# Differences of weights, convolution and recurrence in the first mixer on VectorE, the recurrence's constants on GpSimd

## The chip, the cores and the metric

The kernel runs on one core of a Trainium2 chip. The metric is device time in microseconds (us), taken as the median of three runs of the whole program. Beside it stands one profiled execution, whose trace gives the time of single instructions. The engines are named as the profile names them: PE is TensorE, DVE is VectorE, ACT is ScalarE, POOL is GpSimd, SP is SyncE (which here only issues transfers), PEld is TensorE's load of weights.

## What is computed

Two layers, each a token mixer and a squared-ReLU feed-forward block, on one sequence of 1024 tokens with 1024 features. Before every block the activations are normalised and then scaled and shifted by vectors that come from a conditioning vector `c` (adaLN). The first layer's mixer is the one that matters here, a Griffin recurrent block:

```python
u = h @ w_in
xb, gb = jnp.split(u, 2, axis=-1)
gate = jax.nn.gelu(gb)
xc = conv(xb, conv_w) + conv_b                      # 4 taps along the sequence, per feature
r = sigmoid(blockwise(xc, wr) + br)
i = sigmoid(blockwise(xc, wi) + bi)
log_a = -8 * r * softplus(-lam)
a = exp(log_a)
b = sqrt(-expm1(2 * log_a)) * (i * xc)
hs = scan(hs * a + b)                               # along the sequence
return (hs * gate) @ w_out
```

Everything is float32. D_RNN is 1280, in five blocks of 256 features.

## The kernel before

Activations lie transposed, 128 features on the partitions and 512 tokens (one half of the sequence) along a tile. A float32 product is made of three products of a shorter type, fp32r: a value v is split into vh, its rounding, and vl = v - vh, the **difference**, and `mm3` (lines 351 to 353) adds wh·xh, wh·xl and wl·xh. So each weight tile and each activation that goes into a product costs a rounding, always on ACT, and a difference on some other engine. Which engine makes the difference is the subject of this case:

- `weights` (line 334) loads a raw tile of 128x1024 by SP (line 325; three buffers), rounds it on ACT (line 328), and makes the difference on POOL or DVE, by a rotating list `self.lo`: `[1]`, which holds during the first layer, is POOL every time. Differences that are needed a second time are written to memory (line 346) and loaded again for the second half (line 330).
- `startup` computes the scale A0 and shift S0 of the first norm by eight steps kt. In each, `mac` (lines 551, 553) is a chain of eight DVE operations on 128x128 tiles, which PE transposes (line 566) to give the shift (line 569); `cols` (lines 560, 563) gives the scale. Then `apply1` with `first=True` makes the normalised input: a product on POOL (line 97), two scalings on ACT (98, 99), a difference on DVE (100). The differences of these first weights are POOL's too (line 581).
- `mixer0` runs by a list of steps, `plan`: "c" is a convolution (`conv`), "g" a gate, "l" the recurrence (`lru`), "o" the output projection (`oproj`), with the block and the half. Between steps, one or two DVE operations of a later conditioning vector are put in (line 458). `conv` drains a product out of PSUM by three DVE operations (642), rounds it on ACT (647) and makes the difference on POOL (648). `lru` ends with a chain on DVE: 696, 697, a square root on ACT (699), 703, the scan (705), the gate (708), then the rounding on ACT (710) and the difference on POOL (711). `oproj` multiplies that and adds into the activations on DVE (729), which frees the PSUM buffer.
- `lru_params` makes the constants of the recurrence, some 30 tiny operations on tiles of 128x10 and 128x20, nearly all on DVE (lines 390 to 416).

The order on each engine is not the order of the code: a scheduler sorts the instructions of all steps and engines when the program is built, and each engine then works through its own list strictly in order. An instruction that waits holds up all that stand behind it on its engine.

Of the kernel before, what the change touches and what calls it, by code (L numbers as in the profile page):

```python
# [9 lines left out]
FT = mybir.dt.float32  # L10
# [37 lines left out]
class Norm:  # L48
# [39 lines left out]
        else:  # L88
            self.rstd = ps

    def apply1(self, kt, A, sh, first=False):
        T, nc = self.T, self.T.nc
        t = T.nshort()
        hh, hl = T.tileR(), T.tileR()
        a, b = A[:, kt:kt + 1], sh[:, kt:kt + 1]
        if first:
            nc.gpsimd.tensor_tensor(t, T.x[self.h, kt], self.rstd, op=OP.mult)
            nc.scalar.activation(hh, t, AF.Identity, bias=b, scale=a)
            nc.scalar.activation(t, t, AF.Identity, bias=b, scale=a)
            nc.vector.tensor_tensor(hl, t, hh.bitcast(FT), op=OP.subtract)  # L100
        else:
            nc.vector.scalar_tensor_tensor(t, T.x[self.h, kt], a, self.rstd, op0=OP.mult, op1=OP.mult)  # L102
            nc.scalar.activation(hh, t, AF.Identity, bias=b)  # L103
            nc.vector.scalar_tensor_tensor(hl, t, b, hh.bitcast(FT), op0=OP.add, op1=OP.subtract)  # L104
        return hh, hl

    def apply(self, A, sh):
# [95 lines left out]
class Trunk:  # L203
# [182 lines left out]
    def lru_params(self):  # L386
        nc, col = self.nc, self.col

        hb = self.const.tile([P, 20], FT, name="hb")
        nc.vector.tensor_scalar(hb, col[:, 186:206], 0.5, None, op0=OP.mult)  # L390
        self.hbr = lambda k: hb[:, k:k + 1]
        self.hbi = lambda k: hb[:, 10 + k:11 + k]

        lam = col[:, 206:216]
        v = nc.vector
        w = [self.small([P, 10], f"sp{k}", 1) for k in range(6)]
        ab, u, z, z2, acc, mx = w
        v.tensor_scalar(ab, lam, -1.0, None, op0=OP.mult)
        v.tensor_tensor(ab, ab, lam, op=OP.max)
        nc.scalar.activation(u, ab, AF.Exp, scale=-1.0)  # L400
        v.tensor_scalar(z, u, 2.0, None, op0=OP.add)
        v.reciprocal(z, z)
        v.tensor_tensor(z, z, u, op=OP.mult)
        v.tensor_tensor(z2, z, z, op=OP.mult)
        v.memset(acc, 1.0 / 17)
        for k in (15, 13, 11, 9, 7, 5, 3, 1):
            v.tensor_tensor(acc, acc, z2, op=OP.mult)
            v.tensor_scalar(acc, acc, 1.0 / k, None, op0=OP.add)
        v.tensor_tensor(acc, acc, z, op=OP.mult)
        v.tensor_scalar(mx, lam, -1.0, 0.0, op0=OP.mult, op1=OP.max)  # L410

        sp = self.const.tile([P, 20], FT, name="sp")
        v.tensor_scalar(acc, acc, 2.0, None, op0=OP.mult)
        v.tensor_tensor(acc, acc, mx, op=OP.add)
        v.tensor_scalar(sp[:, 0:10], acc, 4.0, None, op0=OP.mult)
        v.tensor_scalar(sp[:, 10:20], acc, -4.0, None, op0=OP.mult)
        self.sp = lambda k: sp[:, k:k + 1]
        self.nsp = lambda k: sp[:, 10 + k:11 + k]
# [77 lines left out]
    def startup(self, pool, norm, normb):  # L496
# [77 lines left out]
        mac(0)  # L574
        cols(0)
        for kt in range(KT):
            h.append(norm.apply1(kt, A0, S0, first=True))
            wh = self.wp.tile([P, 768], FR, name=self.nm("wh"), tag="wh")
            wl = self.wp.tile([P, 768], FR, name=self.nm("wl"), tag="wl")
            A.copy(wh, wt[kt][:, 0:768])  # L580
            nc.gpsimd.tensor_tensor(wl, wt[kt][:, 0:768], wh.bitcast(FT), op=OP.subtract)
            if kt + 1 < KT:
                mac(kt + 1)
            for f in range(6):
                if f == 3 and kt + 1 < KT:
                    cols(kt + 1)
                s = slice(f * P, (f + 1) * P)
                self.mm3(acc[f], (wh[:, s], wl[:, s]), h[kt], kt == 0, kt == KT - 1)
# [21 lines left out]
    def mixer0(self, hx, g1, tail, first, plan):  # L610
# [21 lines left out]
        def conv(u, h, pss=None):  # L632
            pss = pss or proj(wcols(u * 256), h)
            for j in range(2):
# [10 lines left out]
                    V.tensor_tensor(y[:, 0:3], y[:, 0:3], edge[:, f], op=OP.add)  # L645
                yh, yl = self.tileR(), self.tileR()
                A.copy(yh, y)
                G.tensor_tensor(yl, y, yh.bitcast(FT), op=OP.subtract)
                xc[u, j], xcs[u, j] = y, (yh, yl)

        def edges():
# [21 lines left out]
        def lru(u, h):  # L673
# [26 lines left out]
            for m in range(2):  # L700
                f = 2 * u + m
                a, b = ab[m]
                V.tensor_tensor(b, b, v[m], op=OP.mult)
                hs = self.tmp("hs")
                V.tensor_tensor_scan(hs, a, b, 0.0 if h == 0 else last[:, f:f + 1], op0=OP.mult, op1=OP.add)
                if h == 0:
                    V.tensor_copy(last[:, f:f + 1], hs[:, HT - 1:HT])
                V.scalar_tensor_tensor(hs, hs, 0.5, gt[u, m], op0=OP.mult, op1=OP.mult)
                yh, yl = self.tileR(), self.tileR()
                A.copy(yh, hs)  # L710
                G.tensor_tensor(yl, hs, yh.bitcast(FT), op=OP.subtract)  # L711
                Y[u, h, m] = (yh, yl)

        def oproj(us, h):
# [543 lines left out]
    def run(self):  # L1258
# [48 lines left out]


        self.layer = 0
        N["m0", 0], N["m0", 1] = Norm(self, 0), Norm(self, 1)  # L1310
        with ExitStack() as st:
            hm[0], first = self.startup(pool(st, "start", 9), N["m0", 0], N["m0", 1])
        F = FFN(self, 0, None, hf)
        with ExitStack() as st:
# [33 lines left out]
                    "g21", "c31", "o011", "l21", "g31", "c41", "l31", "g41", bA, "o21", nA, "l41", f1a, "o341", f1b]  # L1348
            self.mixer0(hm, lambda: mod[0, 2], sqs("f0"), first, plan)
            self.drain()  # L1350


            F.g2, F.tail = mod[0, 5], tail
# [200 lines left out]
```

## Time and profile before

| | |
|---|---|
| median of three runs | 2579.44 us (2574.14 to 2582.48) |
| the profiled execution's own time | 2578.01 us |
| its span, first to last instruction | 2576.2 us |
| PE busy | 2437.7 us, 95% |
| DVE, ACT, POOL busy | 1513.0, 1233.1, 969.9 us |
| mean granted clock of TensorE | 0.978 |

A busy time counts what the engine shows as running, with time in which an instruction has begun and cannot go on. Idle time is put down to what came last of the things waited for. Because PE is busy for nearly the whole span, only the places where it is not matter for the end: the stretch from 0 to 360 us, with the startup, the first half of the mixer and part of the second, is where most of them lie.

### The profile page before, as it was taken

The numbers are of one execution on the slowest core, as the hardware profiler recorded it, in microseconds if no ns is written. First come the engines' busy times: TensorE is split into PE (matmuls) and PEld (weight loads), VectorE is DVE, ScalarE is ACT, GpSimd is POOL, SyncE is SP. The second block draws the span as 40 slices with busy tenths as digits, with TensorE's granted clock in tenths as the row PEclk, the third lists the DMA queues.
The fourth block names the chain that finished last, engine by engine and source line by source line (L and its number), as shares of the span: only waits on it lengthen the run. The fifth ranks groups of instructions, "written<-read, shape, count | busy, mean of one in ns | idle before, by whom it ended". The sixth has DMA issues, their size and how long they took to land. (4 is left out here: it accounts for less than half of the span.)

```text
span 2576.2 us, 30961 instructions
## 1 busy us (share of the span) xinstructions
PE 2437.7 (95%) x10954; PEld 1966.9 (76%) x10954; DVE 1513.0 (59%) x2837; ACT 1233.1 (48%) x2188; POOL 969.9 (38%) x575
## 2 busy tenths in 40 slices
PE   7888999998999999999997999999998999999999
PEld 6666778776788888888776777888886877788887
DVE  6688855788844411376687876555558876321112
ACT  3545565631121133235546767768743974433322
POOL 3455411222122234230137932322325994344442
PEclk8889999999999999999998999999999999999999
DMA  7466566336511378654431431222240104322231
GB/s 238 164 222 202 171 216 227 106 131 222 178 49 47 115 263 298 243 176 164 147 107 30 172 98 64 96 87 90 97 133 9 34 27 146 115 90 97 84 104 60
DMA packets 212285, 342.53 MB, mean 133 GB/s; under 512 B 19658, under 2 KB 123298, under 8 KB 212130
## 3 DMA queue, kind: packets, MB, share of 16 engines
q1 hardware_dynamic: 183184, 295.29, 33.8%
q10 hardware_dynamic: 28946, 45.27, 5.3%
q8 instruction: 86, 1.41, 0.2%
q14 instruction: 69, 0.57, 0.1%
HBM read 274.97 MB, written 65.54 MB: 132 GB/s over the span
## 5 line engine op out<-in xcount | busy, mean ns | idle before, releaser
L334 POOL TENSOR_TENSOR wl<-raw,wh 128x1024 fp32r<-128x1024 f32 (+2 forms) x233 | 572.2, 2463 | 1108.2 <-ACT wh L328 1063.6
L328 ACT CAST wh<-raw 128x1024 fp32r<-128x1024 f32 (+2 forms) x296 | 304.8, 1032 | 584.8 <-PE ps L352 226.5
L351 PE MATMUL ps<-a,wh 128*128 128x512 f32 x1152 | 464.0, 405 | 30.2 <-DVE a L729 12.4
L352 PE MATMUL ps<-a,wh 128*128 128x512 f32 x1152 | 461.1, 400 | 2.9 <-POOL a L711 1.5
L353 PE MATMUL ps<-a,wl 128*128 128x512 f32 x1152 | 459.9, 400 | 0.7 <-DMA wl<-part 0.7
L351 PE MATMUL pd<-a,wh 128*128 128x512 f32 x1072 | 430.1, 402 | 10.5 <-ACT g L667 4.3
L352 PE MATMUL pd<-a,wh 128*128 128x512 f32 x1072 | 430.2, 401 | 7.2 <-DVE a L104 3.7
L353 PE MATMUL pd<-a,wl 128*128 128x512 f32 x1072 | 429.3, 400 | 0.0
L174 DVE SCALAR_TENSOR_TENSOR a<-ps,mod,a 128x512 f32<-128x512 f32 x352 | 259.9, 746 | 262.2 <-PE ps L353 261.5
L351 PEld LDWEIGHTS ps<-a,wh 128*128 128x128 f32 x1152 | 219.5, 191 | 86.1 <-DVE a L729 13.3
L352 PEld LDWEIGHTS ps<-a,wh 128*128 128x128 f32 x1152 | 220.0, 191 | 56.0 <-POOL a L711 2.8
L353 PEld LDWEIGHTS ps<-a,wl 128*128 128x128 f32 x1152 | 219.5, 191 | 54.5 <-DMA wl<-part 1.6
L351 PEld LDWEIGHTS pd<-a,wh 128*128 128x128 f32 x1072 | 203.7, 190 | 62.3 <-issue 5.1
L352 PEld LDWEIGHTS pd<-a,wh 128*128 128x128 f32 x1072 | 204.8, 191 | 58.6 <-DVE a L104 5.0
L353 PEld LDWEIGHTS pd<-a,wl 128*128 128x128 f32 x1072 | 204.5, 191 | 49.2
L1147 POOL TENSOR_SCALAR s<-s,rr 128x128 f32<-128x128 f32 (+7 forms) x128 | 225.8, 1779 | 34.6 <-DVE rr L1145 27.3
L351 PE MATMUL ps<-hid,wh 128*128 128x512 f32 x512 | 204.4, 399 | 11.2 <-DVE a L174 8.0
L352 PE MATMUL ps<-hid,wh 128*128 128x512 f32 x512 | 203.1, 397 | 0.0
L353 PE MATMUL ps<-hid,wl 128*128 128x512 f32 x512 | 203.1, 397 | 0.0
L1025 ACT ACTIVATE signs<-sc,tc 128x384 int8<-128x384 f32 (+5 forms) x186 | 164.0, 882 | 77.6 <-DVE tc L1040 66.4
L458 DVE SCALAR_TENSOR_TENSOR a<-a,cond,a 128x512 f32<-128x512 f32 x140 | 133.0, 983 | 36.7 <-DMA a<-in_ada_w_dram 36.2
L152 DVE TENSOR_TENSOR a<-r,a 128x512 fp32r<-128x512 f32 x64 | 46.9, 754 | 141.6 <-ACT a L151 140.4
(274 smaller groups left out, 3748.9 us busy)
## 6 DMA issues: line engine op xcount, KB each, us to landing
raw<-in_ffn_w_dram SPq DMA_DIRECT2D x192, 512.0 KB, 3.7
a<-in_ada_w_dram ACTq DMA_DIRECT2D x160, 256.0 KB, 3.4
part<-wl SPq DMA_DIRECT2D x69, 512.0 KB, 3.4
wl<-part SPq DMA_DIRECT2D x69, 512.0 KB, 4.1
part<-wh SPq DMA_DIRECT2D x40, 512.0 KB, 2.7
wh<-part SPq DMA_DIRECT2D x40, 512.0 KB, 3.5
raw<-in_a_w_in_dram SPq DMA_DIRECT2D x34, 512.0 KB, 4.3
raw<-in_a_w_out_dram SPq DMA_DIRECT2D x20, 512.0 KB, 4.2
```

Source lines behind the costliest of these rows:

```text
L152: nc.any.tensor_tensor(ql, r, qh.bitcast(FT), op=OP.subtract)
L174: nc.vector.scalar_tensor_tensor(xt, ps, self.g2[:, m:m + 1], xt, op0=OP.mult, op1=OP.add)
L328: nc.scalar.copy(wh, raw)
L334: eng.tensor_tensor(wl, raw, wh.bitcast(FT), op=OP.subtract)
L351: pe.matmul(out, wh, xh, start=start, stop=False)
L352: pe.matmul(out, wh, xl, start=False, stop=False)
L353: pe.matmul(out, wl, xh, start=False, stop=stop)
L458: nc.vector.scalar_tensor_tensor(a, r, s, a, op0=OP.mult, op1=OP.add)
L1025: A.activation(self.signs[:, 0:L], sc, AF.Sign, bias=0.0 if neg is None else neg.bitcast(FT), accum_out=n)
L1147: G.tensor_scalar(sl[e][:, 0:L], sl[e][:, 0:L], r[:, e:e + 1], None, op0=OP.mult)
```

## The change

All of the differences in the first layer up to the end of the mixer are made by DVE: those of the startup's weights (581), of the weights in `weights` (`self.lo` is `[0]` from the start until the mixer is drained, and `[1]` again after), of the convolution (648) and of the recurrence's output (711). `apply1` loses its special form for the first half: it takes the form that all other norms have, two DVE operations and one ACT operation. The tiny operations of `lru_params` go to POOL, 27 of them; three stay on DVE.

```diff
-    def apply1(self, kt, A, sh, first=False):
+    def apply1(self, kt, A, sh):
...
-        if first:
-            nc.gpsimd.tensor_tensor(t, T.x[self.h, kt], self.rstd, op=OP.mult)
-            nc.scalar.activation(hh, t, AF.Identity, bias=b, scale=a)
-            nc.scalar.activation(t, t, AF.Identity, bias=b, scale=a)
-            nc.vector.tensor_tensor(hl, t, hh.bitcast(FT), op=OP.subtract)
-        else:
-            nc.vector.scalar_tensor_tensor(t, T.x[self.h, kt], a, self.rstd, op0=OP.mult, op1=OP.mult)
-            nc.scalar.activation(hh, t, AF.Identity, bias=b)
-            nc.vector.scalar_tensor_tensor(hl, t, b, hh.bitcast(FT), op0=OP.add, op1=OP.subtract)
+        nc.vector.scalar_tensor_tensor(t, T.x[self.h, kt], a, self.rstd, op0=OP.mult, op1=OP.mult)
+        nc.scalar.activation(hh, t, AF.Identity, bias=b)
+        nc.vector.scalar_tensor_tensor(hl, t, b, hh.bitcast(FT), op0=OP.add, op1=OP.subtract)
...
-        nc.vector.tensor_scalar(hb, col[:, 186:206], 0.5, None, op0=OP.mult)
+        nc.gpsimd.tensor_scalar(hb, col[:, 186:206], 0.5, None, op0=OP.mult)
...
-        v = nc.vector
+        v = nc.gpsimd
...
-        v.tensor_tensor(ab, ab, lam, op=OP.max)
+        nc.vector.tensor_tensor(ab, ab, lam, op=OP.max)
...
-        v.reciprocal(z, z)
+        nc.vector.reciprocal(z, z)
...
-        v.tensor_scalar(mx, lam, -1.0, 0.0, op0=OP.mult, op1=OP.max)
+        nc.vector.tensor_scalar(mx, lam, -1.0, 0.0, op0=OP.mult, op1=OP.max)
...
-            nc.gpsimd.tensor_tensor(wl, wt[kt][:, 0:768], wh.bitcast(FT), op=OP.subtract)
+            V.tensor_tensor(wl, wt[kt][:, 0:768], wh.bitcast(FT), op=OP.subtract)
...
-                G.tensor_tensor(yl, y, yh.bitcast(FT), op=OP.subtract)
+                V.tensor_tensor(yl, y, yh.bitcast(FT), op=OP.subtract)
...
-                G.tensor_tensor(yl, hs, yh.bitcast(FT), op=OP.subtract)
+                V.tensor_tensor(yl, hs, yh.bitcast(FT), op=OP.subtract)
...
         self.layer = 0
+        self.lo = [0]
...
             self.drain()
+            self.lo = [1]
```

The scheduler sorts anew. In the changed kernel a line's number is lower by 6 (the scan of line 705 is line 699 there). Two places show what moves.

VectorE, the second recurrence (block 1, first half), before: from the sum for the root (696) to the gated output (708). Names are those of the program, with the buffer's number.

```order
L696 SCALAR_TENSOR_TENSOR v_1191<-v_1191,tg_1223 128x512
L703 TENSOR_TENSOR tg_1208<-tg_1208,v_1191 128x512
L703 TENSOR_TENSOR tg_1232<-tg_1232,v_1191 128x512
L705 SCALAR_TENSOR_TENSOR hs_1242<-la_1210,tg_1208 128x512
L705 SCALAR_TENSOR_TENSOR hs_1251<-la_1234,tg_1232 128x512
L707 COPY hlast<-hs_1242 128x1
L668 SCALAR_TENSOR_TENSOR g_1330<-g_1330,pd_1281 128x512
L708 SCALAR_TENSOR_TENSOR hs_1242<-hs_1242,g_975 128x512
```

VectorE, the same place in the changed kernel.

```order
L328 TENSOR_TENSOR wl_1527<-raw_1523,wh_1526 128x1024
L690 SCALAR_TENSOR_TENSOR v_1183<-v_1183,tg_1215 128x512
L328 TENSOR_TENSOR wl_1563<-raw_1559,wh_1562 128x1024
L697 TENSOR_TENSOR tg_1200<-tg_1200,v_1183 128x512
L697 TENSOR_TENSOR tg_1224<-tg_1224,v_1183 128x512
L699 SCALAR_TENSOR_TENSOR hs_1234<-la_1202,tg_1200 128x512
L699 SCALAR_TENSOR_TENSOR hs_1243<-la_1226,tg_1224 128x512
L701 COPY hlast<-hs_1234 128x1
L460 TENSOR_REDUCE adat_1431<-ps_1432 128x4
L702 SCALAR_TENSOR_TENSOR hs_1234<-hs_1234,g_967 128x512
```

Two differences of weights (L328) now stand ahead of the recurrence's end, one of them where DVE waits for the root on ACT; between the products by the root and the gated output no difference stands.

VectorE, the fourth recurrence (block 3, first half), before: around its scans. L729 frees a PSUM buffer of an output projection, L102 belongs to the second half's norm.

```order
L102 SCALAR_TENSOR_TENSOR ns_2136<-a_851,mod_89,ps_2036 128x512
L703 TENSOR_TENSOR tg_1896<-tg_1896,v_1879 128x512
L703 TENSOR_TENSOR tg_1920<-tg_1920,v_1879 128x512
L705 SCALAR_TENSOR_TENSOR hs_1930<-la_1898,tg_1896 128x512
L705 SCALAR_TENSOR_TENSOR hs_1939<-la_1922,tg_1920 128x512
L707 COPY hlast<-hs_1930 128x1
L668 SCALAR_TENSOR_TENSOR g_2018<-g_2018,pd_1969 128x512
L708 SCALAR_TENSOR_TENSOR hs_1930<-hs_1930,g_1757 128x512
L707 COPY hlast<-hs_1939 128x1
L729 SCALAR_TENSOR_TENSOR a_134<-ps_2052,mod_759,a_134 128x512
```

VectorE, the same place in the changed kernel.

```order
L96 SCALAR_TENSOR_TENSOR ns_2128<-a_843,mod_89,ps_2028 128x512
L723 SCALAR_TENSOR_TENSOR a_134<-ps_2044,mod_751,a_134 128x512
L96 SCALAR_TENSOR_TENSOR ns_2134<-a_850,mod_89,ps_2028 128x512
L697 TENSOR_TENSOR tg_1888<-tg_1888,v_1871 128x512
L697 TENSOR_TENSOR tg_1912<-tg_1912,v_1871 128x512
L699 SCALAR_TENSOR_TENSOR hs_1922<-la_1890,tg_1888 128x512
L699 SCALAR_TENSOR_TENSOR hs_1931<-la_1914,tg_1912 128x512
L701 COPY hlast<-hs_1922 128x1
L662 SCALAR_TENSOR_TENSOR g_2010<-g_2010,pd_1961 128x512
L702 SCALAR_TENSOR_TENSOR hs_1922<-hs_1922,g_1749 128x512
```

The first addition into the activations (L723, before L729), which stood behind both scans, stands ahead of them now.

## Rows read from the trace of the kernel before

**Rows 1.** Page, part 2: busy tenths in 40 slices of 64.4 us, PE and DVE

```profile
PE   7888999998999999999997999999998999999999
DVE  6688855788844411376687876555558876321112
```

**Rows 2.** Table by stretch: stretch, its length, then busy us and instructions by engine, clock

```profile
core 0: us, PE busy (x) PEld busy (x) DVE busy (x) ACT busy (x) POOL busy (x), PEclk, DMA share, GB/s
...
150.00:180.00 30.00, 21.30 (x79) 16.61 (x80) 22.94 (x21) 15.44 (x20) 18.63 (x8) 0.77 0.71 241
...
240.00:270.00 30.00, 20.20 (x76) 14.95 (x74) 27.73 (x32) 14.55 (x20) 15.70 (x7) 0.83 0.48 158
270.00:300.00 30.00, 28.48 (x122) 22.95 (x123) 29.38 (x38) 18.23 (x27) 11.66 (x6) 1.00 0.41 140
...
sum 360.00, PE 305.67 PEld 244.00 DVE 270.59 ACT 183.19 POOL 155.58; mean PE 25.47 PEld 20.33 DVE 22.55 ACT 15.27 POOL 12.96
```

**Rows 3.** Groups on DVE, 0 to 360 us: count, busy us, mean ns, idle before

```profile
L458 DVE SCALAR_TENSOR_TENSOR a<-a,cond,a 128x512 f32<-128x512 f32 x42 | 51.0, 1243 | 14.9 <-DMA a<-in_ada_w_dram 14.8
...
L705 DVE TENSOR_TENSOR_SCAN hs<-la,tg 128x512 f32<-128x512 f32 x10 | 24.7, 2510 | 0.0
...
L697 DVE SCALAR_TENSOR_TENSOR tg<-tg,xc 128x512 f32<-128x512 f32 x12 | 13.2, 1104 | 0.9 <-ACT tg L688 0.9
```

**Rows 4.** Single lines on DVE, whole span: least, median, greatest ns

```profile
L458 DVE SCALAR_TENSOR_TENSOR a<-a,cond,a x140: 734/747/2900, 116.4 to 691.6; 128x512 f32<-128x512 f32 x140
...
L697 DVE SCALAR_TENSOR_TENSOR tg<-tg,xc x20: 679/684/2901, 123.3 to 495.1; 128x512 f32<-128x512 f32 x20
...
L705 DVE TENSOR_TENSOR_SCAN hs<-la,tg x10: 1193/3322/3429, 134.8 to 294.0; 128x512 f32<-128x512 f32 x10
...
L334 DVE TENSOR_TENSOR wl<-raw,wh x34: 834/1226/3122, 1316.7 to 1941.6; 128x1024 fp32r<-128x1024 f32 x31, 128x768 fp32r<-128x768 f32 x2, 128x656 fp32r<-128x656 f32 x1
```

**Rows 5.** Groups on POOL, 0 to 360 us

```profile
L334 POOL TENSOR_TENSOR wl<-raw,wh 128x1024 fp32r<-128x1024 f32 x35 | 92.7, 2663 | 82.5 <-ACT wh L328 62.8 <-DMA a<-in_ada_w_dram 14.3 <-DMA raw<-in_a_gate_i_w_dram 3.5
L648 POOL TENSOR_TENSOR a<-xc,a 128x512 fp32r<-128x512 f32 x14 | 18.5, 1325 | 29.7 <-ACT a L647 24.5 <-ACT halo L639 5.2
L711 POOL TENSOR_TENSOR a<-hs,a 128x512 fp32r<-128x512 f32 x12 | 16.2, 1362 | 42.1 <-ACT a L710 42.1
```

**Rows 6.** Instructions in order of time: start us, duration us; startup, DVE and PE

```profile
17.54 1.85 DVE L551 TENSOR_SCALAR ma<-st,cond 128x128 f32<-128x128 f32 x1
...
23.31 1.96 DVE L553 SCALAR_TENSOR_TENSOR ma<-st,cond,ma 128x128 f32<-128x128 f32 x1
...
26.15 0.34 DVE L553 SCALAR_TENSOR_TENSOR ma<-st,cond,ma 128x128 f32<-128x128 f32 x1
...
28.57 0.48 PE L566 MATMUL ps<-ident,ma 128*128 128x128 f32 x1 [5.71 <-DVE ma L553]
...
31.13 1.22 PE L351 MATMUL pd<-a,wh 128*128 128x512 f32 x2 [0.58 <-ACT a L98]
```

**Rows 7.** In order of time, around PE's longest wait in the mixer, 154 to 175 us

```profile
154.80 2.90 DVE L697 SCALAR_TENSOR_TENSOR tg<-tg,xc 128x512 f32<-128x512 f32 x1
157.62 3.55 DVE L458 SCALAR_TENSOR_TENSOR a<-a,cond,a 128x512 f32<-128x512 f32 x2
...
163.89 8.98 POOL L334 TENSOR_TENSOR wl<-raw,wh 128x1024 fp32r<-128x1024 f32 x3 [3.92 <-ACT wh L328]
...
164.11 6.62 DVE L705 TENSOR_TENSOR_SCAN hs<-la,tg 128x512 f32<-128x512 f32 x2
...
174.12 0.80 PE L351 MATMUL ps<-a,wh 128*128 128x512 f32 x1 [8.70 <-ACT a L710]
```

**Rows 8.** In order of time, around the next long wait, 243 to 256 us

```profile
243.52 2.88 DVE L696 SCALAR_TENSOR_TENSOR v<-v,tg 128x512 f32<-128x512 f32 x1
...
248.84 4.47 DVE L705 TENSOR_TENSOR_SCAN hs<-la,tg 128x512 f32<-128x512 f32 x2
...
255.33 0.79 PE L351 MATMUL ps<-a,wh 128*128 128x512 f32 x1 [7.97 <-DVE a L729]
```

**Rows 9.** Groups on DVE, whole span: differences of weights

```profile
L334 DVE TENSOR_TENSOR wl<-raw,wh 128x1024 fp32r<-128x1024 f32 x31 | 44.0, 1420 | 25.2 <-ACT wh L328 25.0
```

More of the change, by code (lines that the diff above doesn't have):

```diff
@@ L576, in startup @@
         for kt in range(KT):
-            h.append(norm.apply1(kt, A0, S0, first=True))
+            h.append(norm.apply1(kt, A0, S0))
             wh = self.wp.tile([P, 768], FR, name=self.nm("wh"), tag="wh")
```

## The prediction, made before the changed kernel ran

> **What bounds the kernel now.** I read the slices first [rows 1]. PE is at 9 tenths or more nearly everywhere; its weakest run of slices is the first four, which end at 258 us, and in these DVE is at 6 to 8 tenths. The second view is the table by stretch [rows 2]: over the first 360 us PE is busy 305.67 us, so it stands idle for 54.3, and DVE is busy 270.59, so it has 89.4 us free. The holes are not spread evenly. From 150 to 180 us PE is busy 21.30 of 30, from 240 to 270 it is 20.20, and in just these two the granted clock is low, 0.77 and 0.83, where the stretch from 270 to 300 has 1.00. So a hole costs more than its length: when PE comes back after it, its products run at the lower of its two levels (1.2 GHz instead of 2.4) for some microseconds.
>
> Third, what the holes wait for, in order of time. The longest ends at 174.12: PE waited 8.70 us for ACT's rounding of the second recurrence's output [rows 7]. The next ends at 255.33: 7.97 us for an addition on DVE (L729) that frees a PSUM buffer and stood behind two scans [rows 8]. Both end in a chain on DVE, and the last view says why that chain is slow. One scan takes 1.19 us at the least, but 3.32 in the median, and the mean over the first 360 us is 2.51 [rows 3, 4]. The operation of L458 is the same every time and takes 0.747 in the median, 2.900 at most; over the first 360 us the mean is 1.243. What happens in the long ones is seen at one place: from 163.89 POOL works 8.98 us at three differences of weights, and two scans that begin at 164.11 take 6.62 [rows 7]. DVE's operations with two inputs from SBUF begin, and then stand until a POOL instruction is through. So in this stretch much of DVE's busy time is standing, and it is POOL's differences that it stands for.
>
> **The change, part by part.** *VectorE's load.* Added over the first 360 us [rows 5]: 35 differences of 128x1024, 14 of L648, 12 of L711, and in the startup 8 of 128x768 and 8 operations more in `apply1`. On DVE a difference of 128x1024 takes 1.226 us (L334, median), an operation of 128x512 0.684 (L697, median) [rows 4]; for 128x768 I take the middle, 0.95. That is 35 x 1.226 + 34 x 0.684 + 8 x 0.95 = 73.8 us. Given back is the standing: L458 42 x (1.243 - 0.747) = 20.8, the scans 10 x (2.51 - 1.193) = 13.2, L697 12 x (1.104 - 0.684) = 5.0 [rows 3, 4], so 39 us from three groups alone. L553, L696, L703 and others show the same long cases among their short ones (1.96 beside 0.34 for L553 [rows 6], 2.88 for L696 [rows 8]); I estimate 30 for them. And some 27 tiny operations leave. So DVE's load stays about the same, within 10 us either way, and that by itself brings nothing. What changes is where it lies: DVE's chains become as short as their own operations, and the differences stand elsewhere in the order.
>
> *Startup.* The first product in full begins at 31.13 us. It needs the first shift, hence the chain of eight (L551, L553), which began at 17.54 and was through at 28.57, though one link costs 0.34 [rows 6]: 3 us of work in 11. Two links took 1.85 and 1.96 beside POOL's operations, and the tiny operations stood in between. Now POOL has only tiny ones then. The gain is at most 11 - 3 = 8, less what stands in the chain's way now (one operation of `apply1`, 0.68, and one difference of 0.95); and POOL's 27 tiny operations can still hold DVE, each briefly. ACT's chain is one operation shorter in each of the eight steps. I take 5 (bounds: -2, if the tiny ones hold each link, and 8).
>
> *The hole to 174.12.* In the chain before it, L697 took 2.90, two of L458 3.55, two scans 6.62 [rows 7]; at the medians and the least scan of rows 4 they are 0.68, 1.49 and 2.39, so 8.5 us go. In the same piece of the order there stand now two differences of weights and one of a convolution, 2 x 1.226 + 0.684 = 3.1, one of them while DVE waits for the root. The output comes 5.4 to 6.6 us sooner, and PE's 8.70 fall to about 3; of the time at the low clock about 2 us go with it (the first product after the hole takes 0.80, and the stretch's clock is 0.77 [rows 2]). Gain 8 (bounds 0 and 11).
>
> *The hole to 255.33.* L696 took 2.88, the two scans 4.47 [rows 8], so 2.2 and 2.1 us of standing, with an L458 of the same kind ahead of them. More important is the order: the addition that PE waits for stands ahead of the scans now. PE gets on with the next piece, of six products, and then waits for the second addition, behind the scans. Of 7.97 I take 5, and 2 for the clock (0.83): 7 (bounds 0 and 10).
>
> *The rest to 360 us.* What remains of the 54.3 is the first 30 us, which wait for data, and some ten waits of 1 to 4 us. From 270 to 300 DVE is busy 29.38 of 30 [rows 2], so it is the bound there, and there the standing is the largest part of L458. I take 4 (bounds 0 and 12).
>
> *The price.* A difference waits for ACT's rounding. On POOL that held up only POOL, which had time: 82.5 us idle ahead of the weights' differences alone [rows 5]. On DVE it holds up everything behind. Where DVE makes such differences already, later in the program, it stood idle 25.2 us for 31 of them [rows 9], 0.8 each. 77 are moved within the first 360 us: 62 us, which the 89.4 of idle time can hold, but not at every place. I take 3 (bounds 0 and the rival's 42).
>
> *Behind 360 us.* The order of PE is the same from the end of the mixer on, apart from names, and PE is at 9 tenths; what is gained stays gained. What the 18 differences that follow cost or give I put at nothing: DVE is at 5 tenths in the two slices up to 451 us, which hold most of them [rows 1].
>
> Sum: 5 + 8 + 7 + 4 - 3 = 21. The profiled execution took 2578.01, of which 1.8 lie outside its span; it is 1.4 below the median of the runs, 2579.44. So 2578 - 21 = **2557**. A measurement of this kernel tells 0.3%, 7.7 us, from no change.
>
> **The rivals.** *1. VectorE's order stalls (slower).* The place is the list of DVE between 90 and 360 us: each difference stands at the head and waits for a rounding, which waits for a raw tile, and the additions and drains that free PE's buffers stand behind. It decides from where the waits take all of the idle time and the gain: (89.4 + 24) / 77 = 1.5 us each. At 1.7 each, 131 - 89 - 24 = 18 us are lost: **2596**. For it: 29.38 of 30 busy at 270 to 300 [rows 2], and L648 and L711 follow a rounding that ACT makes just before. Against: 0.8 each where it can be seen [rows 9], and the scheduler puts other work between. In the same direction goes a rule of the Trainium skill (Perfetto Trace Analysis, section "Optimizing Scalar/DVE Operations"): a saturated DVE is a reason to take work off it, even to GpSimd. By that rule alone, with no relief, DVE would have 73.8 us more to do than before and nearly fill the stretch. The section adds that the two share a read port of SBUF, so that moving work between them may not help; the row that decides is the scan of 2.51 against 1.19 [rows 3, 4], which shows the sharing, and so I don't give this more weight than 0.1.
>
> *2. The holes form again elsewhere.* DVE's load is the same, so PE may wait for it just as long at other places; only the startup's 5 stays: **2573**. For it: DVE's sum, above. Against: the two long holes hang on chains of a few operations, not on a sum, and one of them is undone by the order itself.
>
> *3. The holes close.* The holes to 174 and 255 go entirely with their clock (11 + 10), the startup gives 8, the rest 10: 39 us, **2539**. For it: POOL's differences were slow too (2.66 us for 1.23), and what waits for them comes sooner, the loads of the raw tiles among them. Against: DVE is nearly full at 270 to 300.
>
> **How the numbers follow.** The forecast has 0.53, by its own bounds 2546 to 2568; rival 1 0.10, rival 2 0.17, rival 3 0.20. Faster by over 0.3%, that is under 2571.7: nearly all of the forecast (0.51), rival 3, and a third of rival 2 (0.06): 0.77. Slower: rival 1, 0.10. The rest, 0.13, is no difference. The range for 8 in 10 reaches from rival 3's better half to beyond rival 2: 2537 to 2577.
>
> **What would show it.** Right: over the first 360 us the mean of a scan falls to about 1.2 and of L458's operation to about 0.75, DVE's busy time stays within 10 us of 270, POOL's falls under 20; the wait for the second recurrence's output is under 4 us, and the clock of that stretch is over 0.9; the first full product begins before 29 us. Wrong: the means fall and PE's idle time to the end of the mixer does not (rival 2), or DVE's idle time ahead of L334, L648 and L711 is over 1.5 us each (rival 1); or the scans stay long, and then it was not POOL that they stood for.

## The result and the profile after

The changed kernel took 2551.82 us (median of four runs, 2549.04 to 2558.93), the kernel before beside it 2580.96 (four runs, 2574.14 to 2584.48). The ratio is 0.9895 with a 95% interval of 0.9877 to 0.9913: 29 us faster, with an interval of 22 to 32. The forecast was 2557, in a range from 2537 to 2577.

The profiled execution of the changed kernel is the slowest of its four, 2558.93 (span 2557.0); the profiled one of before took 2578.01. So the two traces show 19 of the 29 us, and of the rest they can say nothing.

The slices of the changed kernel, PE and DVE, against [rows 1]:

```profile
PE   7998999999999999999987999999998999999999
DVE  5888775788643412566677876555558875321212
```

In the first four slices PE has 7 9 9 8 where it had 7 8 8 8, and DVE 5 8 8 8 where it had 6 6 8 8. The stretches that answer to [rows 2]:

```profile
core 0: us, PE busy (x) PEld busy (x) DVE busy (x) ACT busy (x) POOL busy (x), PEclk, DMA share, GB/s
150.00:180.00 30.00, 30.00 (x133) 24.05 (x132) 28.48 (x44) 14.05 (x21) 0.00 (x0) 1.00 0.49 159
240.00:270.00 30.00, 19.77 (x70) 15.47 (x70) 28.25 (x42) 16.79 (x23) 0.00 (x0) 0.77 0.26 83
270.00:300.00 30.00, 28.80 (x123) 22.90 (x122) 18.29 (x28) 11.31 (x16) 0.00 (x0) 1.00 0.66 226
0.00:360.00 360.00, 319.00 (x1392) 257.08 (x1393) 273.26 (x481) 191.24 (x283) 12.57 (x36) 0.94 0.65 214
```

Over 360 us PE is busy 13.3 us more, DVE 2.7 us more, and POOL has 12.57 us left of 155.58. DVE got through 481 instructions in that time (405 before, by the same view). The stretch from 150 to 180 has no hole and a clock of 1.00; the stretch from 240 to 270 has a hole as long as before (PE busy 19.77 us where it was 20.20).

DVE's groups over the first 360 us, the first three against [rows 3], the others moved here from POOL [rows 5]:

```profile
L452 DVE SCALAR_TENSOR_TENSOR a<-a,cond,a 128x512 f32<-128x512 f32 x48 | 34.8, 748 | 27.8 <-DMA a<-in_ada_w_dram 27.8
...
L699 DVE TENSOR_TENSOR_SCAN hs<-la,tg 128x512 f32<-128x512 f32 x10 | 11.7, 1206 | 0.0
...
L691 DVE SCALAR_TENSOR_TENSOR tg<-tg,xc 128x512 f32<-128x512 f32 x14 | 9.6, 683 | 0.5 <-ACT tg L682 0.5
...
L328 DVE TENSOR_TENSOR wl<-raw,wh 128x1024 fp32r<-128x1024 f32 x35 | 42.3, 1215 | 1.4 <-ACT wh L322 1.4
...
L642 DVE TENSOR_TENSOR a<-xc,a 128x512 fp32r<-128x512 f32 x16 | 11.0, 685 | 3.8 <-ACT a L641 3.8
...
L705 DVE TENSOR_TENSOR a<-hs,a 128x512 fp32r<-128x512 f32 x12 | 8.2, 683 | 1.1 <-ACT a L704 1.1
```

Each mean is now the undisturbed one: the scan 1206 ns (2510 before), the sums of L452 748 (1243), L691 683 (1104). DVE waited 6.3 us in all for the roundings that the moved differences need (last column of the last three rows), 0.1 us for each of their 63.

Where the lead was made is read from PE's waits. A row has the time at which a product begins, and in brackets how long PE had waited for it and for what. Before, beside those that end at 31.13, 174.12 and 255.33 [rows 6 to 8]:

```profile
97.19 0.77 PE L351 MATMUL pd<-a,wh 128*128 128x512 f32 x1 [4.26 <-ACT g L667]
...
149.90 0.47 PE L351 MATMUL pd<-a,wh 128*128 128x512 f32 x1 [3.53 <-DVE xc L642]
...
313.92 0.50 PE L351 MATMUL ps<-a,wh 128*128 128x512 f32 x1 [1.84 <-DVE a L729]
...
472.43 0.80 PE L351 MATMUL ps<-a,wh 128*128 128x512 f32 x1 [4.43 <-DVE adat L466]
```

And in the changed kernel:

```profile
25.89 1.22 PE L345 MATMUL pd<-a,wh 128*128 128x512 f32 x2 [1.48 <-ACT a L97]
...
82.10 0.76 PE L345 MATMUL pd<-a,wh 128*128 128x512 f32 x1 [3.99 <-DVE xc L636]
...
138.17 0.77 PE L345 MATMUL pd<-a,wh 128*128 128x512 f32 x1 [5.44 <-DVE xc L636]
...
230.56 0.50 PE L345 MATMUL ps<-a,wh 128*128 128x512 f32 x1 [3.77 <-DVE a L723]
...
258.58 0.79 PE L347 MATMUL pd<-a,wl 128*128 128x512 f32 x1 [9.61 <-DVE wl L328]
...
294.55 0.47 PE L345 MATMUL ps<-a,wh 128*128 128x512 f32 x1 [1.20 <-DVE a L723]
...
450.06 0.77 PE L345 MATMUL ps<-a,wh 128*128 128x512 f32 x1 [2.90 <-DVE adat L460]
```

The lead is the time by which the changed kernel begins the same product sooner. It is 5.2 us at the first full product (31.13 to 25.89), 15.1 at the first wait in the mixer (97.19 to 82.10), 11.7 at the next (149.90 to 138.17). The wait that ended at 174.12 has no counterpart. The steps between come from counting PE's products in the two traces, which have nearly the same order: the lead is 13.6 us where the mixer begins to run without a hole, 11.1 behind the wait that ends at 138.17, 22.0 when the hole to 174.12 is past, 27.5 when the hole to 255.33 is past, 15.9 behind the wait that ends at 258.58, and 20.9 at 360 us. The wait that ends at 258.58 is new; with the products at the lower clock behind it, it takes 11.6 back. At the fifth pair of scans (290.65 to 260.79 by the order of time on DVE) DVE's lead is 29.9, but PE's is 14.6 a little later: the product that begins at 294.55 began at 309.11. At 450 the lead is 22.4, at the end 19.2; no single wait takes the last 3, and it was not sought further.

The new wait, in order of time, ACT's rounding and then DVE (PE's row is the one at 258.58 above):

```profile
219.16 2.01 ACT L322 CAST wh<-raw 128x1024 fp32r<-128x1024 f32 x2
...
251.50 0.74 DVE L98 SCALAR_TENSOR_TENSOR a<-ns,mod,a 128x512 fp32r<-128x512 f32 x1
...
255.99 1.41 DVE L452 SCALAR_TENSOR_TENSOR a<-a,cond,a 128x512 f32<-128x512 f32 x2
257.31 2.35 DVE L328 TENSOR_TENSOR wl<-raw,wh 128x1024 fp32r<-128x1024 f32 x2
```

The weights of the second half's first convolution block are rounded by 221.2, yet their difference is made at 257.3. In DVE's order it stands behind the whole of the second half's norm (16 operations of L96 and L98), and what follows it. The longest wait among those is 1.75 us. The difference is late by its place alone.

### The profile page after: what moved, and what is told of

It is laid out like the page before. It is cut to its first block, busy times and chain, and to the rows that moved or that the text cites. A ratio compares the mean times of both kernels' runs of the same rounds, so it can differ in the third digit from the quotient of the medians.

```text
span 2557.0 us, 30862 instructions
## 1 busy us (share of the span) xinstructions
PE 2435.1 (95%) x10954; PEld 1965.4 (77%) x10954; DVE 1502.1 (59%) x2905; ACT 1227.8 (48%) x2180; POOL 797.6 (31%) x507
## 5 line engine op out<-in xcount | busy, mean ns | idle before, releaser
L328 POOL TENSOR_TENSOR wl<-raw,wh 128x1024 fp32r<-128x1024 f32 (+2 forms) x194 | 470.7, 2433 | 1186.2 <-ACT wh L322 1169.3
L345 PE MATMUL pd<-a,wh 128*128 128x512 f32 x1072 | 431.2, 404 | 12.2 <-DVE xc L636 9.4
L347 PEld LDWEIGHTS pd<-a,wl 128*128 128x128 f32 x1072 | 204.8, 191 | 60.7 <-DVE wl L328 11.1
L452 DVE SCALAR_TENSOR_TENSOR a<-a,cond,a 128x512 f32<-128x512 f32 x140 | 113.5, 840 | 40.7 <-DMA a<-in_ada_w_dram 40.3
```

Of the source, the lines that this page charges most:

```text
L328: eng.tensor_tensor(wl, raw, wh.bitcast(FT), op=OP.subtract)
L345: pe.matmul(out, wh, xh, start=start, stop=False)
L347: pe.matmul(out, wl, xh, start=False, stop=stop)
L452: nc.vector.scalar_tensor_tensor(a, r, s, a, op0=OP.mult, op1=OP.add)
```

## The experiments

There are two theories. An instruction of VectorE that has begun and cannot go on is called standing. **Theory 1, interference**: a GpSimd instruction that reads SBUF makes VectorE's instructions with two inputs there stand, so each difference taken off GpSimd gives VectorE time, wherever it stands. **Theory 2, the chain**: what counted was only what TensorE waited for, GpSimd's slow and queued differences in the recurrence and the startup; the weights were ready anyway. Each run has its own runs of the kernel before beside it, on the same chip (medians 2580.58, 2580.87 and 2581.36 in the three sets).

### Parts of the change alone

**Startup alone** (on the kernel before):

```diff
-            h.append(norm.apply1(kt, A0, S0, first=True))
+            h.append(norm.apply1(kt, A0, S0))
...
-            nc.gpsimd.tensor_tensor(wl, wt[kt][:, 0:768], wh.bitcast(FT), op=OP.subtract)
+            V.tensor_tensor(wl, wt[kt][:, 0:768], wh.bitcast(FT), op=OP.subtract)
```

> The kernel before with the startup's part alone: the norm's first application in VectorE's form and the startup's eight weight differences on VectorE; all else on GpSimd as before. Theory 1 (interference: a GpSimd difference lengthens what VectorE does beside it, wherever it stands): first full product before 27 us, the 56 steps of the startup's chain nearer 343 than 518 ns, 6 to 12 us less in all, 2569 to 2575. Theory 2 (chain: only what TensorE waits for counts): the first product 5 us earlier, the chain's steps as before, 2574 to 2577.

Measured 2574.81, ratio 0.998 (0.997 to 0.999): 6 us, where the two expectations meet. The startup's chain is nearly free of standing: the 56 steps take 382 ns each (518 before), which theory 2 did not expect, and the first full product begins at 25.48 us. In the trace the lead is about 12 us from the second recurrence to 550 us, and 6.0 at the end; where the other half goes was not sought.

```profile
L547 DVE SCALAR_TENSOR_TENSOR ma<-st,cond,ma 128x128 f32<-128x128 f32 x56 | 20.2, 382 | 0.1
```

**Weights alone**:

```diff
+        self.lo = [0]
         N["m0", 0], N["m0", 1] = Norm(self, 0), Norm(self, 1)
...
             self.drain()
+            self.lo = [1]
```

> The kernel before with the 35 weight differences of the mixer on VectorE alone; the startup, the convolution's and the recurrence's differences and the constants as before. Theory 1 (interference): the scans come down from 2510 ns towards 1200 to 1500, the steps of the weights' sums from 1243 towards 800 to 900, and this part brings most, 10 to 18 us: 2563 to 2571. Theory 2 (chain): the weights were ready ahead of their products anyway, TensorE waited for the recurrence's differences in GpSimd's queue, which is shorter now but still there: 0 to 6 us less, 2575 to 2581.

Measured 2554.99, ratio 0.9907 (0.9893 to 0.9921): 26 us, more than theory 1 expected, and nearly the whole of the change. Theory 2 had at most 6. The groups over 360 us, line numbers as before:

```profile
L458 DVE SCALAR_TENSOR_TENSOR a<-a,cond,a 128x512 f32<-128x512 f32 x48 | 36.5, 783 | 23.0 <-DMA a<-in_ada_w_dram 22.7
...
L705 DVE TENSOR_TENSOR_SCAN hs<-la,tg 128x512 f32<-128x512 f32 x10 | 11.7, 1205 | 0.0
```

With the convolution's and the recurrence's 28 differences still on GpSimd the scans are undisturbed: it was the weights' differences that they stood for.

**Convolution and recurrence alone** (lines 648 and 711, `G` to `V`):

```diff
-                G.tensor_tensor(yl, y, yh.bitcast(FT), op=OP.subtract)
+                V.tensor_tensor(yl, y, yh.bitcast(FT), op=OP.subtract)
...
-                G.tensor_tensor(yl, hs, yh.bitcast(FT), op=OP.subtract)
+                V.tensor_tensor(yl, hs, yh.bitcast(FT), op=OP.subtract)
```

> The kernel before with the convolution's and the recurrence's differences (28 of them) on VectorE alone; the weights' 35 stay on GpSimd. Theory 1 (interference): the weights' differences still lengthen VectorE's work, which has got more of it, scans stay over 2000 ns, 0 to 6 us less: 2575 to 2581. Theory 2 (chain): TensorE's wait at 174 us, three differences of GpSimd long, is gone, and this part brings most, 8 to 16 us: 2565 to 2573.

Measured 2576.33, ratio 0.998 (0.9969 to 0.9991): 4 us, within theory 1 and outside theory 2.

```profile
L705 DVE TENSOR_TENSOR_SCAN hs<-la,tg 128x512 f32<-128x512 f32 x10 | 22.6, 2298 | 0.0
```

The scans stay long. The wait that had ended at 174.12 is shorter by 3 us and another, 12.2 us for the addition of L729, ends at 259.0 in place of the 7.97 at 255.33: more work on a DVE that still stands.

**Constants alone** (`v = nc.gpsimd` in `lru_params`, with the three operations that stay on VectorE):

```diff
-        v = nc.vector
+        v = nc.gpsimd
```

> The kernel before with the recurrence's constants on GpSimd alone. They are some 30 instructions of 128x10 (0.1 to 0.4 us each) at the start, on neither theory in TensorE's way: both expect no change, 2577 to 2584; with GpSimd's queue at its longest at the start, up to 5 us slower if the constants delay the startup's weight differences behind them.

Measured 2592.12, ratio 1.005 (1.0035 to 1.0065): 12 us slower, a miss for both theories, which had at most 5. The startup's chain got slower, 660 ns a step where it was 518 before (first row: constants alone, second: before, both up to 90 us):

```profile
L553 DVE SCALAR_TENSOR_TENSOR ma<-st,cond,ma 128x128 f32<-128x128 f32 x56 | 36.2, 660 | 1.1
...
L553 DVE SCALAR_TENSOR_TENSOR ma<-st,cond,ma 128x128 f32<-128x128 f32 x56 | 28.9, 518 | 1.0
```

That is 7 us of DVE's time, but the loss does not lie there. By the same product PE is 2.8 us behind in the first half of the mixer, and level again at 185 us, since its wait for the second recurrence, 8.70 us before, is 3.39. The loss comes with a new wait for the gate's operation (L670):

```profile
239.16 0.79 PE L351 MATMUL pd<-a,wh 128*128 128x512 f32 x1 [8.01 <-DVE g L670]
```

DVE had fallen behind by then, though PE had not: the third pair of scans begins at 219.28, before at 212.15. PE is 10.8 us behind after this wait, 9.0 at 360 us and 18.1 at the end of this trace. Why DVE falls behind, and where the rest goes, was not settled.

**Constants undone** in the changed kernel, where everything else stays as changed:

```diff
-        v = nc.gpsimd
+        v = nc.vector
```

> The changed kernel with the recurrence's constants back on VectorE, the rest as changed. Alone on the kernel before, the constants on GpSimd cost 11 us, where GpSimd still had the startup's differences behind them; with those gone GpSimd has nothing else to do, so theory 1 expects no loss from them in the change: within 4 us of the change's 2552, either side, with up to 2 us slower for some 7 us more of work on VectorE at the start. If the cost of the constants is their own (GpSimd slower at them than VectorE, and something waits for them), undoing them gains 5 to 12 us: 2540 to 2547.

Measured 2555.86 (2544.89 to 2558.43), ratio 0.9894 (0.9877 to 0.9911), the change's own ratio. So the constants cost nothing that can be told once GpSimd's other differences are gone. The 12 us come only where both are on GpSimd; by what way is not shown, since the order on every engine is sorted anew as well.

The gains alone, 6, 26 and 4 us, come to 36, with the constants' loss to 24; together the parts make 29 (22 to 32). As the constants lose nothing in the change, the three gains overlap, or their uncertainties (2 to 4 us each) add up to the rest. The traces, one of each, speak for an overlap: in the first half of the mixer PE leads by 12.6 us with the startup alone, by 5.3 with the weights alone, and by 13.6 with everything.

### GpSimd's reading given back, with nobody waiting for it

In the changed kernel, behind each weight difference on VectorE, GpSimd makes the same difference again over the loaded weights, which nothing reads any more:

```diff
         eng.tensor_tensor(wl, raw, wh.bitcast(FT), op=OP.subtract)
+        if self.lo == [0] and self.layer == 0:
+            nc.gpsimd.tensor_tensor(raw, raw, wh.bitcast(FT), op=OP.subtract)
```

> The changed kernel, and behind each of the mixer's weight differences on VectorE the same difference once more on GpSimd, over the loaded weights, which nothing reads any more: GpSimd gets its 93 us of reading back, nobody waits for a result, only the loaded weights' buffer comes free later. Theory 1 (interference by reading): scans and the weights' sums lengthen again (scan from 1206 to over 1700 ns, the sums from 748 to over 900), 8 to 20 us slower than the change: 2560 to 2572. Theory 2 (chain: GpSimd's differences counted only where TensorE waited for them): the change's time within 3 us, 2549 to 2555.

The control writes the same buffer twice and reads nothing:

```diff
+        if self.lo == [0] and self.layer == 0:
+            for c in (0.0, 1.0):
+                nc.gpsimd.memset(raw, c)
```

> The control to the one before: the same buffer, held as long or nearly, but written twice by GpSimd with a constant and not read. Theory 1 (interference by reading): scan and sums stay at 1206 and 748 ns, the change's time within 4 us: 2548 to 2556. A rival within theory 1 (any access of GpSimd, or the later release of the buffer, costs it): as slow as the run that reads, 2560 to 2572.

And once more with one input read:

```diff
+        if self.lo == [0] and self.layer == 0:
+            nc.gpsimd.tensor_scalar(raw, wh.bitcast(FT), 0.5, None, op0=OP.mult)
```

> The run with repeated differences on GpSimd once more, with one input read there in place of two (the rounded weights times a constant, written over the loaded ones). If any read of GpSimd interferes with VectorE's instructions of two SBUF inputs: scans and sums lengthen by about as much as they overlap with it, 10 to 35 us slower than the writing control's 2552: 2562 to 2587. If it takes two inputs on both sides: scan 1206 and sums 748 ns as in the control, 2549 to 2556.

Measured: reading two inputs 2586.87, ratio 1.0027 (1.0017 to 1.0037); writing alone 2552.5, ratio 0.9892 (0.9873 to 0.9911); reading one input 2563.13, ratio 0.9935 (0.9921 to 0.995). The control is the change's time; the reading run loses all of the gain and more, 34 us against its control, though no result of GpSimd is waited for. That is more than theory 1 expected (2560 to 2572), though the scans lengthened less than it expected (to a mean of 1416 ns, not over 1700). Theory 2 is out: the interference costs wherever it lengthens VectorE's work, which TensorE then waits for in many places. Groups over 360 us, the run that reads two inputs:

```profile
L328 DVE TENSOR_TENSOR wl<-raw,wh 128x1024 fp32r<-128x1024 f32 x35 | 56.5, 1621 | 0.0
L454 DVE SCALAR_TENSOR_TENSOR a<-a,cond,a 128x512 f32<-128x512 f32 x42 | 37.7, 926 | 8.9 <-DMA a<-in_ada_w_dram 8.9
L699 DVE TENSOR_TENSOR tg<-tg,v 128x512 f32<-128x512 f32 x12 | 18.5, 1581 | 1.7 <-ACT v L695 1.7
L725 DVE SCALAR_TENSOR_TENSOR a<-ps,mod,a 128x512 f32<-128x512 f32 x24 | 17.6, 744 | 4.1 <-PE ps L349 4.1
...
L701 DVE TENSOR_TENSOR_SCAN hs<-la,tg 128x512 f32<-128x512 f32 x10 | 13.8, 1416 | 0.0
...
L330 POOL TENSOR_TENSOR raw<-raw,wh 128x1024 f32<-128x1024 f32 x35 | 98.3, 2816 | 208.8 <-DVE wl L328 168.9 <-issue 27.3 <-ACT halo L635 6.4
```

The control:

```profile
L455 DVE SCALAR_TENSOR_TENSOR a<-a,cond,a 128x512 f32<-128x512 f32 x48 | 34.9, 747 | 17.8 <-DMA a<-in_ada_w_dram 17.6 <-DVE tg L694 0.2
L726 DVE SCALAR_TENSOR_TENSOR a<-ps,mod,a 128x512 f32<-128x512 f32 x24 | 17.7, 744 | 2.0 <-PE ps L350 2.0
...
L700 DVE TENSOR_TENSOR tg<-tg,v 128x512 f32<-128x512 f32 x14 | 9.0, 685 | 6.4 <-ACT v L696 6.4
...
L331 POOL MEMSET raw<- 128x1024 f32 x70 | 66.4, 955 | 201.8 <-DVE wl L328 124.2 <-issue 52.7 <-ACT a L644 15.9
```

Compare the same lines in both. The sums and the products by the root, with two inputs from SBUF, go from 747 to 926 and from 685 to 1581 ns. The additions (L725, L726), which read one input from PSUM, take 744 in both. And 66 us of GpSimd that only writes lengthen nothing. That agrees with a rule of the Trainium skill (SBUF — State Buffer, section "Who interferes with whom"): a VectorE instruction with two SBUF inputs contends with a GpSimd instruction that reads SBUF, not with one that only writes it. That the loaded weights' buffer comes free later is no rival for the 34 us: the differences of L328 waited 0.0 us for a rounding in the run that reads.

With one input read, the interference is there but smaller, 11 us against the control, though GpSimd is busy longer and holds the buffer longer (first two rows; the third is the changed kernel's):

```profile
L330 POOL TENSOR_SCALAR raw<-wh 128x1024 f32<-128x1024 f32 x35 | 108.6, 3115 | 180.6 <-DVE wl L328 163.4 <-issue 12.4 <-ACT halo L635 3.5
...
156.09 3.12 DVE L701 TENSOR_TENSOR_SCAN hs<-la,tg 128x512 f32<-128x512 f32 x2
...
150.65 2.33 DVE L699 TENSOR_TENSOR_SCAN hs<-la,tg 128x512 f32<-128x512 f32 x2
```

Two scans beside it take 3.12, where the changed kernel's take 2.33 and those beside two-input differences took 6.62 [rows 7]. The mean of the scans is no lower than with two inputs read (1445 against 1416 ns); what is shorter is the rest, the sums at 784 ns, the products by the root at 755, the weights' differences at 1320 (1621 with two).

### The new wait at 258.6

**Two differences given back to GpSimd** (those of the weights that TensorE waits for):

```diff
-        self.lo = [0]
+        self.lo = [0] * 25 + [1, 1] + [0] * 33
```

> The changed kernel with two of the 35 weight differences given back to GpSimd: those of the second half's first convolution block, the first of which TensorE waited for 9.6 us, to 258.6 us, behind 17 instructions of the norm in VectorE's order. If the wait is one for VectorE's order alone, GpSimd has the difference done some 3 us after the weights' cast at 227 us, the wait goes to what is late next (the recurrence's second product or the norm, 2 to 5 us), and 4 to 8 us are gained: 2544 to 2548. If something else is late there by then, or VectorE is the bound from 220 to 260 us, 0 to 3 us: 2549 to 2552.

**The same two left on VectorE, asked for ahead of the norm**:

```diff
             if callable(step):
+                if plan[k + 1:k + 2] == ["l40"]:
+                    pre = wcols(0)
                 step()
+            elif step == "c01":
+                conv(0, 1, proj(pre, 1))
```

> The changed kernel with the same two weight differences left on VectorE, but the block's weights asked for ahead of the norm's application in the program. By VectorE's order alone: the wait to 258.6 us shrinks by what stood ahead, 4 to 8 us gained, 2544 to 2548. If VectorE is the bound there the norm's application comes 2.4 us later in its place and the wait stays under another name: 2549 to 2554.

Measured 2545.49, ratio 0.9863 (0.9843 to 0.9884), and 2544.49, ratio 0.9862 (0.9841 to 0.9882); the control of the section above, from the same set of runs and equal to the change, had 2552.5. So 7 and 8 us are gained (the first run's times, 2539 to 2553, overlap the control's, 2550 to 2557; the second's, 2541 to 2547, don't), and the wait was one for the place in VectorE's order. (The weights were rounded by 221.2, not at 227 as the expectation has it.) The stretch in the second of them:

```profile
240.00:270.00 30.00, 28.25 (x112) 22.65 (x113) 24.72 (x36) 18.16 (x24) 0.00 (x0) 0.90 0.40 135
```

PE 28.25 of 30 in place of 19.77, and the clock 0.90 in place of 0.77.

With the constants on VectorE again (the edit of the run with the constants undone, on top of this one):

> The changed kernel with the weights of the second half's first block asked for before the norm (2544 us) and the constants back on VectorE. If the two are independent: the same step from 2544 as the run with the constants alone makes from 2552, 2540 to 2548.

Measured 2546.25, ratio 0.9867 (0.9852 to 0.9883): no difference from 2544, as in the changed kernel.

### A version that beats both

The weights asked for ahead of the norm, and `self.lo` left at `[0]` through the first layer's feed-forward:

```diff
             self.drain()
-            self.lo = [1]
```

> The changed kernel with those weights asked for before the norm, and the weight differences of the first layer's feed-forward stages (after 360 us) on VectorE too. TensorE is busy 97% of the time from 360 to 900 us in the changed kernel, so there is little to gain: 0 to 4 us less than 2544; where VectorE's waits in order for weights come ahead of what TensorE needs, up to 5 us more: 2540 to 2549.

Measured 2534.11 (2529.09 to 2535.66), ratio 0.9821 (0.9808 to 0.9833): 10 us less than 2544 and 47 less than before, where at most 4 was expected. The sums from 360 to 630 us, with the weights asked for early and then in this run:

```profile
L452 DVE SCALAR_TENSOR_TENSOR a<-a,cond,a 128x512 f32<-128x512 f32 x77 | 65.3, 878 | 12.0 <-DMA a<-in_ada_w_dram 11.8
...
L452 DVE SCALAR_TENSOR_TENSOR a<-a,cond,a 128x512 f32<-128x512 f32 x76 | 54.5, 747 | 12.7 <-DMA a<-in_ada_w_dram 12.4
```

And PE from 630 to 900 us, in the same two:

```profile
630.00:900.00 270.00, 267.05 (x1147) 214.32 (x1146) 120.89 (x162) 60.33 (x82) 67.84 (x28) 1.00 0.32 109
...
630.00:900.00 270.00, 270.00 (x1162) 217.31 (x1162) 142.44 (x188) 60.46 (x82) 0.00 (x0) 1.00 0.34 112
```

PE has no idle time left there. These 3 us are a part of the 10: by the same product this run is ahead of the one before it by 3 us at 360 us, 6 at 940, 8 at 1210 and 11 at the end of the traces. That DVE's sums stood for GpSimd here is shown (878 against 747 ns); which small waits of PE make up the 10 us was not sought.

## Why the prediction was right, and where it was not

- **What bounds the kernel, the standing.** Right, and shown: the means fell as said (scan to 1206, sums to 748), DVE's busy time stayed within 10 us (273.26 against 270.59), and what the run that gives GpSimd its reading back lengthens on DVE are instructions of two SBUF inputs only. That the weights' differences are the cause is shown by the part alone.
- **Startup, 5.** The step that failed is "I take 5", which counts to the first full product and is exact there (5.2); but the lead at the first wait in the mixer is 15, and 13.6 behind it. The ten in between have two halves. From 30 to 100 us PE stood idle 9.5 us before; in the changed kernel, from 30 to 90, 4.5 (length less PE's busy time, by slices of 10 us). The other half is the clock, which the prediction had taken into account at the two long holes and not here. From 30 to 40 us, first before, then after:

```profile
20.00:30.00 10.00, 3.34 (x23) 2.96 (x22) 10.00 (x35) 0.83 (x1) 5.12 (x4) 0.58 0.94 268
30.00:40.00 10.00, 9.35 (x30) 7.90 (x31) 6.28 (x25) 4.60 (x6) 4.37 (x4) 0.50 0.93 278
...
20.00:30.00 10.00, 6.17 (x27) 4.68 (x26) 8.86 (x25) 2.28 (x3) 5.15 (x12) 0.67 1.08 305
30.00:40.00 10.00, 10.00 (x62) 8.60 (x60) 7.58 (x24) 2.89 (x4) 0.00 (x0) 0.99 0.97 265
```

  PE looks busy in both, but before it came out of a slice with 3.34 us of work and ran at 0.50, its lower level, with 30 products in 10 us; now it comes out of one with 6.17 and does 62 at 0.99. (From 40 to 50 us it is the other way about, 51 products at 0.89 before and 44 at 0.66 after, but over the whole way PE needs 5 us less for the same products.)
- **The hole to 174.12, 8.** Right in its mechanism, and too low: the hole closes entirely where 3 us of it were to stay, the clock of its stretch is 1.00, and the lead grows by 10.9 us (11.1 to 22.0), near the bound of 11.
- **The hole to 255.33, 7.** The order was read rightly ("the addition that PE waits for stands ahead of the scans now"), and PE's lead grows by 5.5 us (22.0 to 27.5). The step that failed is the price, "I take 3": 9.61 us of a new wait for a weights' difference, with the low clock behind it, take 11.6 back at this place alone. That is rival 1's place and direction, a difference in VectorE's order, at one point; its mechanism was another. Rival 1, and the price, spoke of a wait for ACT's rounding at 0.8 us each; measured are 6.3 us over 63 of the moved differences, 0.1 each. What costs is the work that stands ahead of a difference which was free to go on an empty engine. The two runs that move it show its price: 7 to 8 us.
- **The rest to 360 us, 4.** Measured is 2.4: 4.9 gained behind the wait that ends at 258.58 (15.9 to 20.9), and 2.5 lost at 138.17 (13.6 to 11.1), where DVE waited 3.19 us for a transfer with the drains of PSUM behind it:

```profile
132.70 1.43 DVE L452 SCALAR_TENSOR_TENSOR a<-a,cond,a 128x512 f32<-128x512 f32 x2 [3.19 <-DMA a<-in_ada_w_dram]
```

- **Behind 360 us, nothing.** By the traces within 4 us: the lead is 20.9 at 360 us, up to 25.0 on the way, 19.2 at the end. The 10 us of the last run are another matter: they come with the feed-forward's differences, which the change leaves on GpSimd.
- **The constants** were counted as "some 27 tiny operations leave". In the change that is right (undone: the same ratio). Alone they cost 12 us. The prediction had allowed for tiny operations that hold each link of the startup's chain (its bound of -2), and that chain did get slower alone, but the loss lies elsewhere.
- **The sum.** 21 forecast, 29 (22 to 32) by the medians, 19 by the traces. That the lead of the traces at 360 us, 20.9, meets the sum of 21 is luck, for the errors of the terms cancel: the startup gave 8.6 more than its 5, the hole to 174 2.9 more than its 8, the hole to 255 1.5 less than its 7, the rest 1.6 less than its 4, and the price was 11.6 at one wait where the prediction had 3 over all.
- **The rule weighed**, which is the Trainium skill's (Perfetto Trace Analysis, section "Optimizing Scalar/DVE Operations": take work off a full DVE, even to GpSimd), speaks against the change if taken by itself. The trace agrees with what the section adds, the read port of SBUF that the two share: with some 74 us of work added, by the prediction's sum, DVE's busy time grew by 2.7.

## What to carry to other kernels

Look at one operation that is always the same, and compare its mean with its median in the stretch that matters: where an operation of two SBUF inputs has 1243 against 747 ns, and one with an input from PSUM has none of that (744 with and without GpSimd's reading), the time is not the engine's work, and moving GpSimd's two-input work onto the engine it disturbs can be free. Then look for the place in the new order: an engine whose order is fixed makes a difference late that waits for nothing, and asking for it earlier in the program was worth as much as a quarter of the change. Try the parts alone where they are independent in the code: here one made nearly all of the gain and another was a loss as long as it stood alone.

## What the runs showed of the hardware that was not expected

- GpSimd's reading costs less with one input read than with two: 35 instructions of 128x1024 beside the mixer cost 34 us with two inputs (2.82 us each) and 11 with one, though these ran longer (3.12 us each). VectorE did not stand through the whole of a one-input instruction: two scans beside one took 3.12 against 2.33 alone, and the longer of the two, 1.99 us, was through at 159.21 when the GpSimd instruction, begun before it at 156.72, went on to 159.87. The page of the Trainium skill named above (SBUF — State Buffer, section "Summary: rules for kernel authors") has the second to issue blocked until the first is through; for one input these rows show less than that.
- GpSimd's writing costs VectorE nothing that these runs can tell: 70 writes of 128x1024 at 0.955 us, the sums at 747 ns, the time of the change.
- Not only instructions of two tiles stood. In the kernel before, 12 instructions that multiply one tile of 128x128 by a column of scalars (L79) lie in the first 360 us. Ten take 271 to 288 ns. The other two began 0.07 us behind a difference on GpSimd; they take 2410 and 1314 ns and end less than 0.1 us after it. In the changed kernel all 12 take 276 to 304. The first of the two:

```profile
112.08 2.41 DVE L79 TENSOR_SCALAR nl<-ident,rs 128x128 f32<-128x128 f32 x1 [0.53 <-POOL rs L76]
```
